# Query heads keep their scale until the exponential, and three gate chunks go ahead of the gate products

## The chip, the cores and the metric

The kernel runs on one core of one Trainium2 chip. The metric is the device time of one execution in microseconds; the time of a version is the median of its runs. One further execution was recorded by the hardware profiler, and every view shown here comes from such a recording. PE is TensorE's matrix unit, PEld its weight loads, DVE is VectorE, ACT is ScalarE, POOL is GpSimd and SP is SyncE, which here only issues transfers.

## The reference, cut to what matters

One layer of a hybrid encoder over 512 tokens of width 2048, in float32. An input projection gives q, k, v, a gate for the attention, and an input and a gate for a recurrent group. Attention has 8 query heads and 2 key/value heads of 128 columns.

```python
q = rms_norm(q.reshape(B, S, N_HEADS, HEAD_DIM), q_norm_w)
k = rms_norm(k.reshape(B, S, N_KV_HEADS, HEAD_DIM), k_norm_w)
q = apply_axial_rope(q, tables)
k = apply_axial_rope(k, tables)
...
s = jnp.einsum('bkgqd,bksd->bkgqs', qb, k_t) * scale
p = jax.nn.softmax(s, axis=-1)
out = jnp.einsum('bkgqs,bksd->bkgqd', p, v_t)
...
mixed = concat([rms_norm(attn_out, attn_norm_w) * silu(g_attn),
                rms_norm(lru_out, lru_norm_w) * silu(g_lru)])
return x + mixed @ w_out
```

Here rms_norm divides a head's 128 values by their root mean square and multiplies by a weight. The root mean square is one number for a token and a head, so it may also be applied to that row of the scores.

## The kernel before

**Matrix products.** Each float32 operand is split into a rounded part ("hi") and the rest ("lo"), both in TensorE's reduced float32 format, and `mm3` (line 151) adds three matmuls: hi·hi, hi·lo, lo·hi. A weight chunk is loaded into one of three `wr` buffers by a transfer that SP issues, ACT rounds it (`wh`, line 223 or 1202) and DVE subtracts (`wl`, line 225 or 1203). A `wr` buffer is free again when that subtraction is done, and the next load into it can be issued only then.

**Stages.** Projection of the recurrent input; the recurrent group itself, laced with further projections; k and v; the two halves of q (`q_proj`, line 1103, four heads each, called from `both`); the attention, laced with gate products (from line 1266); the last gate, the normed output and the output projection. The attention stage runs from about 255 us to 436 us of the profile.

**The heads' norm and rotation.** `norm_rope` (line 541) gets four token tiles with four heads each (two for k). Per tile and head a Square on ACT with an accumulated sum (line 549) gives the sum of squares, `rsqrt_mean` (lines 285 and 286) turns a tile's sums into 1/rms on POOL, and DVE multiplies the tile by it (line 554), multiplies the swapped halves by the sine table in two instructions (line 556), multiplies by the cosine table (line 562) and adds (line 563). The tile `rr` with 1/rms has four buffers.

**The attention.** `attention` (line 667) is a generator with steps d. In a step, PE turns finished weights of two steps before (`turn_weights`, line 631: four transposes and a split by ACT line 578 and DVE line 579, for two token tiles), multiplies weights and values for a head in the even steps (`values`, line 639), turns the q of a later head in the odd ones (`turned`, line 601), and makes two tiles of scores (`weights`, line 607). Each tile of scores goes to `softmax` (line 620): DVE takes the negated maximum of a row (line 623), ACT the exponential with that as its bias and the sum accumulated (line 626), DVE the reciprocal (line 627), POOL the multiplication (line 628). Transposes, scores, turned q and value products share four PSUM banks (`mm`, line 142), in turn: in an odd step two groups of transposes, one turned q and two score tiles take five banks, so the second score tile gets the bank of the first group of transposes.

**The gate products between.** After a score tile PE does one or three units of `gates` (line 1250), four units before the first, as `STEPS` and `weave` say. A unit is six matmuls with 512 columns. Two units make a pair, and the string `PLAN` (line 1248) is the order of the pairs. A `u` is a pair of `gl_units` (line 1159): the recurrent group's gate is formed from seven products of combined blocks, in the order P1, Q6, P2, Q5, Q3, Q7, Q4, of four pairs each. Its weights are 512 KB a pair (two rounded tiles, two subtractions); Q6, Q5, Q3 and Q7 also load 256 KB of combined x (`draw`, line 1172), with one rounding and one subtraction more (`dh` and `dl`, lines 1174 and 1175). A `G` is a pair of `ga_units` (line 1191), the gate of two attention heads: 256 KB, one rounding, one subtraction. An `H` is the same for two more heads. `u` accumulates in the first two of four `pj` banks, `G` and `H` in the other two. From the fifth unit, every second unit also issues a transfer of `out_sums` on POOL's queue, which forms sums of w_out in device memory.

**Who orders what.** PE's order is that of the program. POOL's too, in this stage. ACT, DVE and SP are ordered by a planner from priorities (`tc.high_priority`); each engine then runs its list in order.

Of the kernel before, what the change touches and what calls it, by code (L numbers as in the profile page):

```python
# [11 lines left out]
F32 = mybir.dt.float32  # L12
F32R = mybir.dt.float32r
AF = mybir.ActivationFunctionType
# [3 lines left out]
P = 128  # L18
# [3 lines left out]
NT = SEQ // P  # L22
HD = 128
NH = 8
NKV = 2
G = NH // NKV
# [20 lines left out]
SOON, FIRST = 40, 300  # L47
# [15 lines left out]
def hybrid_kernel(  # L63
# [20 lines left out]
    nc = tc.nc  # L84
# [4 lines left out]
    pools, order = {}, {"left": [], "right": []}  # L89
# [25 lines left out]
    def nm(s):  # L115
        cnt[0] += 1
        return f"{s}_{cnt[0]}"
# [4 lines left out]
    def work():  # L122
        return ("lru", LRU_K2, LRU_B4) if "lru" in pools else ("att", ATT_K2, ATT_B4)

    def k2(dt=F32, shape=(P, SEQ)):
        pool, n, _ = work()
        return pools[pool].tile(list(shape), dt, tag="k2", bufs=n, name=nm("k2"))
# [14 lines left out]
    def mm():  # L142
        return ps.tile([P, SEQ], F32, tag="mm", name=nm("mm"))

    def const(shape, name, dt=F32):
        return cp.tile(list(shape), dt, tag=name, name=name)
# [4 lines left out]
    def mm3(acc, lh, ll, rh, rl, start, stop):  # L151
        nc.tensor.matmul(acc, lh, rh, start=start, stop=False)  # L152
        nc.tensor.matmul(acc, lh, rl, start=False, stop=False)  # L153
        nc.tensor.matmul(acc, ll, rh, start=False, stop=stop)  # L154
# [7 lines left out]
    nc.gpsimd.memset(nhalf, -0.5)  # L162

    nw_st = k2(shape=(KT, P))
    mark = const([P, P], "mark")
    vec_st = const([R_END, P], "vec_st")

    def vec_load():
# [114 lines left out]
    def rsqrt_mean(dst, src, n, width):  # L283

        nc.gpsimd.tensor_scalar(dst, src, 1.0 / n, EPS, op0=ALU.mult, op1=ALU.add)
        nc.gpsimd.tensor_tensor(dst, dst, nhalf[:, :width], op=ALU.pow)
# [75 lines left out]
    def proj_tok(c0, acc):  # L362
        yield from tok_block(acc, w_in, 0, c0, xh, xl, KT)
# [167 lines left out]
    def evac_tok(acc, tile_of):  # L531

        res = []
        with tc.high_priority():
            for t in range(NT):
                e = tile_of()
                nc.scalar.activation(e, acc[t], AF.Identity, scale=rstd[:, t : t + 1])
                res.append(e)
        return res

    def norm_rope(es, nh, tab):

        es = [e[:, : nh * HD].rearrange("p (h d) -> p h d", d=HD) for e in es]
        rs = []
        for e in es:
            r = pools["rot"].tile([P, G], F32, tag="rr", bufs=NT, name=nm("rr"))[:, :nh]
            for h in range(nh):
                sq = pools["rot"].tile([P, HD], F32, tag="sh", bufs=1, name=nm("sh"))
                nc.scalar.activation(sq, e[:, h, :], AF.Square, accum_out=r[:, h : h + 1])  # L549
            rsqrt_mean(r, r, HD, nh)  # L550
            rs.append(r)
        for t, (e, r) in enumerate(zip(es, rs)):
            sq = gbc[:, : nh * HD].rearrange("p (h d) -> p h d", d=HD)
            nc.vector.tensor_mul(e, e, r[:, :, None].broadcast_to([P, nh, HD]))
            for s in range(2):
                nc.vector.tensor_mul(
                    sq.rearrange("p h (a s d) -> p h a s d", s=2, d=32)[:, :, :, s, :],
                    e.rearrange("p h (a s d) -> p h a s d", s=2, d=32)[:, :, :, 1 - s, :],
                    tab[:, t, 1, :].rearrange("p (a s d) -> p a s d", s=2, d=32)[:, None, :, s, :]
                    .broadcast_to([P, nh, 2, 32]),  # L560
                )
            nc.vector.tensor_mul(e, e, tab[:, t, 0, :][:, None, :].broadcast_to([P, nh, HD]))
            nc.vector.tensor_add(e, e, sq)
        return es
# [36 lines left out]
    def turned(rot, h, by=SOON):  # L601

        q = b4(F32R)
        soon(split_ps, turn(rot, h), q[:, 0, :], q[:, 1, :], by=by)
        return q[:, 0, :], q[:, 1, :]

    def weights(q, g, t, by):

        qh, ql = q
        tt = slice(t * P, (t + 1) * P)  # L610
        sc = mm()
        mm3(sc, qh[:, tt], ql[:, tt], kth[g], ktl[g], True, True)
        return soon(softmax, sc, by=by)

    def soon(what, *given, by=SOON):

        with tc.high_priority(by):
            return what(*given)

    def softmax(sc):  # L620

        mx = pools["att"].tile([P, 1], F32, tag="mx", bufs=16, name=nm("mx"))
        nc.vector.tensor_reduce(mx, sc, axis=AX.X, op=ALU.max, negate=True)
        p = k2()
        sm = pools["att"].tile([P, 1], F32, tag="sm", bufs=16, name=nm("sm"))
        nc.scalar.activation(p, sc, AF.Exp, bias=mx, accum_out=sm)
        nc.vector.reciprocal(sm, sm)  # L627
        nc.gpsimd.tensor_scalar(p, p, sm, 0.0, op0=ALU.mult, op1=ALU.add)  # L628
        return p

    def turn_weights(p, t, pth, ptl):
        tt = slice(t * P, (t + 1) * P)
        pt = mm()
        for s in range(NT):
            nc.tensor.transpose(pt[:, s * P : (s + 1) * P], p[:, s * P : (s + 1) * P], ident)  # L635
        p3 = pt.rearrange("p (s q) -> p s q", q=P)
        soon(split_ps, p3, pth[:, :, tt], ptl[:, :, tt])

    def values(h, pth, ptl):

        gs = slice(h // G * HD, (h // G + 1) * HD)
        o = mm()
        for s in range(NT):
            mm3(o, vh[s][:, gs], vl[s][:, gs], pth[:, s, :], ptl[:, s, :], s == 0, s == NT - 1)
        if h % 2 == 0:
            ap_[h // 2] = aring.tile([P, 2, SEQ], F32, name=nm("av"))
        av, asum = ap_[h // 2][:, h % 2, :], sums["a"]
        nc.scalar.copy(av, o)
        if h == 0:
            nc.scalar.activation(asum, av, AF.Square)  # L650
        else:
            sq = k2()
            nc.scalar.activation(sq, av, AF.Square)
            nc.gpsimd.tensor_add(asum, asum, sq)

    def turned_weights():
        return [
            pools["low"].tile([P, NT, SEQ], F32R, tag="pt", bufs=ATT_PT, name=nm("pt"))
            for _ in range(2)
        ]  # L660
# [6 lines left out]
    def attention(rots):  # L667

        pts, ps_ = {0: turned_weights()}, {}
        qs = {h: turned(rots[0], h, FIRST) for h in range(2)}  # L670
        yield 4
        for d in range(2 * NH + 3):
            h, half = divmod(d - 4, 2)
            if h >= 0 and half == 0:
                values(h, *pts.pop(h))
            h, half = divmod(d - 2, 2)
            if 0 <= h < NH:
                if half == 0:
                    pts[h] = pts.get(h) or turned_weights()
                for t in (2 * half, 2 * half + 1):  # L680
                    turn_weights(ps_.pop((h, t)), t, *pts[h])
            h, half = divmod(d, 2)
            if h < NH:
                if half == 1 and h + 2 < NH:
                    qs[h + 2] = turned(rots[(h + 2) // G], (h + 2) % G)
                for e, t in enumerate((2 * half, 2 * half + 1)):
                    ps_[h, t] = weights(qs[h], h // G, t, SOON if d else FIRST)
                    yield STEPS[e]
            elif d < 2 * NH + 2:
                yield 2  # L690
            else:
                yield 0
# [342 lines left out]
    given = {}  # L1035
# [17 lines left out]
    for step in proj_feat(C_XR, a1, first, given):  # L1053
# [8 lines left out]
        c, e = step  # L1062
# [21 lines left out]
    rq, rk = rope_consts()  # L1084
# [16 lines left out]
    rots = []  # L1101

    def q_proj(c0, acc):
        yield from proj_tok(c0, acc)
        rots.append(norm_rope(evac_tok(acc, ev), G, rq))

    def both():
        for n, _ in enumerate(q_proj(C_Q, a4)):
# [127 lines left out]
    def heads_gates(res):  # L1236

        for g in res:
            nc.scalar.activation(g, g, AF.Silu)
        yield  # L1240
        for e, g in enumerate(res):
            dst = ap_[0][:, e, :]
            nc.vector.scalar_tensor_tensor(
                dst, dst, v1(R_AN + e), g, op0=ALU.mult, op1=ALU.mult
            )
            yield

    PLAN = "uuuuG" "uuuuG" "uuuuG" "uuGuuG" "uuGuuG" "uuuuG" "uuuu" "HHHHHHHH"

    def gates():  # L1250
        early, b = [], [pj() for _ in range(4)]
        units = {"u": gl_units(b[:2]), "G": ga_units(0, early, b[2:]), "H": ga_units(1, late, b[2:])}
        todo = iter(())
        for n, unit in enumerate(itertools.chain.from_iterable((u, u) for u in PLAN)):
            done = next(units[unit])
            if n >= 4 and n % 2 == 0:
                next(out_sums, None)
            if done == "Q4":
                todo = itertools.chain(todo, lru_gates(1))
            elif unit == "G" and len(early) == 2 and n == PLAN.rindex("G") * 2 + 1:  # L1260
                todo = itertools.chain(lru_gates(0), heads_gates(early))
# [9 lines left out]
    r = group_rstd([sums["a"]], "r_a", NH * HD)  # L1271
# [31 lines left out]
    acc = []  # L1303
# [74 lines left out]
```

## Time and profile before

| | |
|---|---|
| runs | 649.17, 649.77, 650.11 us; median 649.77 |
| the profiled execution's own time | 650.25 us |
| its span, from the first to the last instruction | 648.1 us |
| mean granted TensorE clock over the span | 0.997 |
| DVE, ACT and POOL busy | 510.2, 379.5 and 136.1 us |
| moved by DMA | 128.19 MB |

The page of a profile gives busy times and the costliest groups of instructions. The view of waits says for whom an engine sat idle. The timeline lists instructions by start, and "x8" is eight of them merged. Matmul ends are modelled and overlap, so PE's speed is read from start to start. The chain of waits goes back from the last instruction, at each step to what released it. The view by stretches gives each engine's busy time and number of instructions, the granted clock, the DMA engines' busy share and GB/s.

### The profile page before, as it was taken

How to read it: one execution, taken by the hardware profiler on the slowest of the kernel's cores; microseconds unless marked ns; L12 is line 12 of the kernel's file. 1: busy time of each engine (PE TensorE's matmuls, PEld its weight loads, DVE VectorE, ACT ScalarE, POOL GpSimd, SP SyncE). 2: the span in 40 equal slices, each digit the busy share in tenths (PEclk: the TensorE clock that was granted, in tenths of full speed). 3: DMA queues.
4: the chain of work that ended last, by engine and by line, in shares of the span. 5: the costliest groups of instructions: out<-in, count | busy, mean ns of one | idle time of the engine just before them, and what ended most of it. 6: DMA issues, size and time to landing. Idle time of an engine off the chain costs nothing.

```text
span 648.1 us, 8952 instructions
## 1 busy us (share of the span) xinstructions
PE 638.3 (98%) x2962; PEld 528.8 (82%) x2962; DVE 510.2 (79%) x894; ACT 379.5 (59%) x699; POOL 136.1 (21%) x173
## 2 busy tenths in 40 slices
PE   8999999999999999979999999999999999999997
PEld 6888888888888888858888888888888888888886
DVE  5877679996799994986768777749937978699994
ACT  3543799489946515765776687745344654443441
POOL 0003303323151300643354334402000000010000
PEclk9999999999999999999999999999999999999999
DMA  8847977897767563597979977853354857586322
GB/s 289 294 135 206 237 199 162 248 251 185 168 181 210 159 209 119 179 271 210 239 214 239 255 217 188 206 147 115 97 182 167 324 167 243 196 280 212 119 95 97
DMA packets 68782, 128.19 MB, mean 198 GB/s; under 512 B 5504, under 2 KB 24320, under 8 KB 68480
## 3 DMA queue, kind: packets, MB, share of 16 engines
q1 hardware_dynamic: 55856, 90.25, 42.5%
q0 software_dynamic: 12704, 37.23, 25.4%
q8 instruction: 23, 0.38, 0.2%
q14 instruction: 23, 0.19, 0.1%
q10 hardware_dynamic: 176, 0.14, 0.1%
HBM read 119.21 MB, written 41.95 MB: 249 GB/s over the span
## 4 chain that ended last, share of the span: by engine, by line
PE 87%; DMA 4%; DVE 3%; ACT 3%; issue 1%; SPq 0%; POOL 0%; ACTq 0%; DVEq 0%
PE pj L152 17%; PE pj L153 17%; PE pj L154 17%; PE mm L984 13%; PE pj L984 11%; PE mm L152 3%; PE mm L154 3%; PE mm L153 3%; DMA wr<-in_w_in_dram 2%; DVE wl L225 1%; PE mm L635 1%; DMA wr<-gs 1%; ACT wh L223 1%; PE mm L255 1%; ACT sh L549 1%
## 5 line engine op out<-in xcount | busy, mean ns | idle before, releaser
L223 ACT CAST wh<-wr 128x512 fp32r<-128x512 f32 x151 | 90.5, 619 | 75.8 <-PE pj L154 30.9
L225 DVE TENSOR_TENSOR wl<-wr,wh 128x512 fp32r<-128x512 f32 (+1 forms) x153 | 105.0, 710 | 26.9 <-ACT wh L223 26.7
L152 PE MATMUL pj<-x,wh 128*128 128x512 f32 x248 | 97.8, 394 | 0.0
L153 PE MATMUL pj<-x,wh 128*128 128x512 f32 x248 | 96.7, 390 | 0.4 <-DVE x L258 0.4
L154 PE MATMUL pj<-x,wl 128*128 128x512 f32 x248 | 96.7, 390 | 0.0
L152 PE MATMUL pj<-wh,x 128*128 128x512 f32 x240 | 94.0, 392 | 0.0
L154 PE MATMUL pj<-wh,x 128*128 128x512 f32 x240 | 93.5, 389 | 0.0
L153 PE MATMUL pj<-wl,x 128*128 128x512 f32 x240 | 93.4, 389 | 0.0
L778 ACT CAST oh<-rw 128x512 fp32r<-128x512 f32 x94 | 56.3, 621 | 38.8 <-PE mm L984 15.5
L779 DVE TENSOR_TENSOR ol<-rw,oh 128x512 fp32r<-128x512 f32 x94 | 61.8, 687 | 10.8 <-ACT oh L778 7.8
L153 PEld LDWEIGHTS pj<-x,wh 128*128 128x128 f32 x248 | 46.6, 188 | 10.1 <-DVE x L258 0.7
L152 PEld LDWEIGHTS pj<-x,wh 128*128 128x128 f32 x248 | 46.6, 188 | 9.8 <-ACT x L257 0.2
L154 PEld LDWEIGHTS pj<-x,wl 128*128 128x128 f32 x248 | 46.5, 188 | 9.8
L154 PEld LDWEIGHTS pj<-wh,x 128*128 128x128 f32 x240 | 45.0, 188 | 9.5
L153 PEld LDWEIGHTS pj<-wl,x 128*128 128x128 f32 x240 | 45.1, 188 | 9.2
L152 PEld LDWEIGHTS pj<-wh,x 128*128 128x128 f32 x240 | 45.1, 188 | 9.1
L984 PE MATMUL mm<-ol,mh 128*128 128x512 f32 (+1 forms) x128 | 49.0, 382 | 0.0
L984 PE MATMUL mm<-oh,ml 128*128 128x512 f32 (+1 forms) x128 | 48.9, 382 | 0.0
L984 PE MATMUL mm<-oh,mh 128*128 128x512 f32 (+1 forms) x128 | 48.9, 382 | 0.0
L916 POOL DMA_DIRECT2D out_dram<-xt x12 | 6.5, 541 | 189.5 <-DVE xt L952 139.1
L628 POOL TENSOR_SCALAR k<-k,sm 128x512 f32<-128x512 f32 x32 | 32.8, 1025 | 61.2 <-DVE sm L627 59.6
L984 PE MATMUL pj<-ol,mh 128*128 128x512 f32 (+1 forms) x104 | 39.7, 382 | 0.0
(238 smaller groups left out, 1342.0 us busy)
## 6 DMA issues: line engine op xcount, KB each, us to landing
wr<-in_w_in_dram SPq DMA_DIRECT2D x59, 512.0 KB, 4.5
rw<-in_w_out_dram SPq DMA_DIRECT2D x63, 256.0 KB, 3.6
gs<-in_w_in_dram POOLq DMA_DIRECT2D x24, 512.0 KB, 6.7
ts<-in_w_out_dram POOLq DMA_DIRECT2D x24, 512.0 KB, 7.8
wr<-gs SPq DMA_DIRECT2D x16, 512.0 KB, 4.7
rw<-ts SPq DMA_DIRECT2D x31, 256.0 KB, 4.4
wr<-in_w_in_dram SPq DMA_DIRECT2D x17, 256.0 KB, 4.5
gs<-gs POOLq DMA_DIRECT2D x8, 512.0 KB, 7.3
```

What stands on the lines that cost most here:

```text
L152: nc.tensor.matmul(acc, lh, rh, start=start, stop=False)
L153: nc.tensor.matmul(acc, lh, rl, start=False, stop=False)
L154: nc.tensor.matmul(acc, ll, rh, start=False, stop=stop)
L223: rounded(hi[:, c], raw[:, k, c])
L225: nc.vector.tensor_sub(lo[:, c], raw[:, k, c], f(hi[:, c]))
L255: nc.tensor.transpose(pt[:, t * P : (t + 1) * P], xc[:, h * n + t, ks], ident)
L549: nc.scalar.activation(sq, e[:, h, :], AF.Square, accum_out=r[:, h : h + 1])
L628: nc.gpsimd.tensor_scalar(p, p, sm, 0.0, op0=ALU.mult, op1=ALU.add)
L778: nc.scalar.copy(hi, src)
L779: nc.vector.tensor_sub(lo, src, f(hi))
L916: (queue or nc.gpsimd).dma_start(of[t * P : (t + 1) * P, os_], xts[g][t][:, cs])
L984: nc.tensor.matmul(bank[key][:, to], lh[:, a, ts_], rh[:, cols], start=i == 0 and j == 0, stop=i == 7 and j == 2,)
```

## The change

Four edits go together. `norm_rope` gets an optional list of tiles for 1/rms; the two calls for q pass tiles of their own (`q_r`, eight of them, kept to the end), and with those given, the tiles of q are not multiplied by 1/rms. `softmax` gets the column of 1/rms of its head and token tile: a new ACT instruction on a 128x1 tile multiplies the negated maximum by it, and the exponential takes it as its scale. `mark`, a tile of which one column is written, gives up the space that the eight tiles take. `PLAN` has three `G` pairs ahead of P1, none inside or after P1 and Q6, and one after P2 and one after Q5; from the 21st pair on it is as before. k is treated as before.

```diff
-    mark = const([P, P], "mark")
+    mark = const([P, P - 16 * NT], "mark")
+    q_r = [const([P, G], f"q_r{i}") for i in range(2 * NT)]
...
-    def norm_rope(es, nh, tab):
+    def norm_rope(es, nh, tab, rs=None):
 
         es = [e[:, : nh * HD].rearrange("p (h d) -> p h d", d=HD) for e in es]
-        rs = []
-        for e in es:
-            r = pools["rot"].tile([P, G], F32, tag="rr", bufs=NT, name=nm("rr"))[:, :nh]
+        given, rs = rs is not None, rs or []
+        for t, e in enumerate(es):
+            if not given:
+                rs.append(pools["rot"].tile([P, G], F32, tag="rr", bufs=NT, name=nm("rr"))[:, :nh])
+            r = rs[t]
             for h in range(nh):
                 sq = pools["rot"].tile([P, HD], F32, tag="sh", bufs=1, name=nm("sh"))
                 nc.scalar.activation(sq, e[:, h, :], AF.Square, accum_out=r[:, h : h + 1])
             rsqrt_mean(r, r, HD, nh)
-            rs.append(r)
         for t, (e, r) in enumerate(zip(es, rs)):
             sq = gbc[:, : nh * HD].rearrange("p (h d) -> p h d", d=HD)
-            nc.vector.tensor_mul(e, e, r[:, :, None].broadcast_to([P, nh, HD]))
+            if not given:
+                nc.vector.tensor_mul(e, e, r[:, :, None].broadcast_to([P, nh, HD]))
...
-    def weights(q, g, t, by):
+    def weights(q, g, t, r, by):
...
-        return soon(softmax, sc, by=by)
+        return soon(softmax, sc, r, by=by)
...
-    def softmax(sc):
+    def softmax(sc, r):
 
         mx = pools["att"].tile([P, 1], F32, tag="mx", bufs=16, name=nm("mx"))
         nc.vector.tensor_reduce(mx, sc, axis=AX.X, op=ALU.max, negate=True)
+        nc.scalar.activation(mx, mx, AF.Identity, scale=r)
         p = k2()
         sm = pools["att"].tile([P, 1], F32, tag="sm", bufs=16, name=nm("sm"))
-        nc.scalar.activation(p, sc, AF.Exp, bias=mx, accum_out=sm)
+        nc.scalar.activation(p, sc, AF.Exp, bias=mx, scale=r, accum_out=sm)
...
-                    ps_[h, t] = weights(qs[h], h // G, t, SOON if d else FIRST)
+                    r = q_r[NT * (h // G) + t][:, h % G : h % G + 1]
+                    ps_[h, t] = weights(qs[h], h // G, t, r, SOON if d else FIRST)
...
-        rots.append(norm_rope(evac_tok(acc, ev), G, rq))
+        n = NT * len(rots)
+        rots.append(norm_rope(evac_tok(acc, ev), G, rq, q_r[n : n + NT]))
...
-    PLAN = "uuuuG" "uuuuG" "uuuuG" "uuGuuG" "uuGuuG" "uuuuG" "uuuu" "HHHHHHHH"
+    PLAN = "GGGuuuu" "uuuu" "uuuuG" "uuuuG" "uuGuuG" "uuuuG" "uuuu" "HHHHHHHH"
```

## The prediction

> **What bounds the kernel now.** I read the page first, then PE's waits, then PE's timeline around the waits, then the chain of waits.
>
> ```profile
> PE 638.3 (98%) x2962; PEld 528.8 (82%) x2962; DVE 510.2 (79%) x894; ACT 379.5 (59%) x699; POOL 136.1 (21%) x173
> ```
>
> PE is busy for 98% of the span. So a change that leaves PE's work alone, as this one does, can only win what PE loses to waits, and what a slower clock after them costs. PE's waits are five:
>
> ```profile
> PE mm L152 <- DVE pt L579: 3.3, 1, 3.3
> PE mm L1023 <- DVE ones L159: 1.0, 1, 1.0
> PE mm L152 <- ACT k L626: 0.9, 1, 0.9
> PE pj L153 <- DVE x L258: 0.4, 1, 0.4
> PE pj L331 <- DVE wh L223: 0.3, 1, 0.3
> ```
>
> Three of them are in the load phase at the start (lines 159, 258 and the first chunk), which the change doesn't touch. The other two, 4.2 us, lie in the attention:
>
> ```profile
> 284.09 0.60 PE L574 MATMUL mm<-ident,ev 128*128 128x128 f32 x4
> 285.62 0.50 PE L152 MATMUL mm<-kt,b 128*128 128x512 f32 x1 [0.93 <-ACT k L626]
> ...
> 287.56 0.39 PE L154 MATMUL pj<-wh,dl 128*128 128x512 f32 x1
> 291.28 0.79 PE L152 MATMUL mm<-kt,b 128*128 128x512 f32 x1 [3.33 <-DVE pt L579]
> ...
> 294.81 0.40 PE L154 MATMUL pj<-wh,dl 128*128 128x512 f32 x1
> 295.04 0.39 PE L152 MATMUL pj<-x,wh 128*128 128x512 f32 x1
> ```
>
> From start to start a matmul takes 0.23 us (294.81 to 295.04). The first wait costs 0.9 to 1.0. The second costs 291.28 - 287.56 - 0.23 = 3.5. Behind it eight matmuls take 294.81 - 291.28 = 3.5 us instead of 8 x 0.23 = 1.8, which is 1.7 more. The view by stretches shows why:
>
> ```profile
> core 0: us, PE busy (x) PEld busy (x) DVE busy (x) ACT busy (x) POOL busy (x), PEclk, DMA share, GB/s
> 285.00:290.00 5.00, 2.33 (x9) 1.61 (x9) 2.13 (x6) 2.32 (x6) 3.68 (x4) 1.00 1.00 346
> 290.00:295.00 5.00, 3.72 (x9) 2.99 (x10) 4.38 (x8) 2.66 (x6) 0.00 (x0) 0.66 1.08 299
> 340.00:360.00 20.00, 20.00 (x99) 16.55 (x99) 15.68 (x28) 12.54 (x27) 8.74 (x10) 1.00 0.95 260
> ```
>
> After the long wait the granted clock is 0.66. In all the place loses 1.0 + 3.5 + 1.7 = 6.2 us, and that is about all that there is to win. Why PE waited stands in the chain:
>
> ```profile
> 262.43 1.27 POOL rr L285
> 263.77 1.02 POOL rr L286
> ...
> 279.44 1.22 DVE wl L225
> 280.68 8.51 DMA wr<-in_w_in_dram
> 289.28 0.63 ACT wh L223
> 289.93 0.69 DVE wl L225
> 290.62 0.61 DVE pt L579
> ```
>
> Read it backwards. The scores at 291.28 wanted a PSUM bank that held transposed weights; DVE had their subtraction (line 579) in its list behind that of a weight chunk (289.93), that chunk had landed at 289.2, its load had been issued only at 280.68, and it was issued so late because DVE freed the buffer only at 280.66. DVE was behind, and POOL's 1/rms for the second half of q was one cause. What DVE did from 255.5 to 287.5, a wait that ends in that stretch being put in whole:
>
> ```profile
> L225 DVE TENSOR_TENSOR wl<-wr,wh 128x512 fp32r<-128x512 f32 x13 | 9.7, 745 | 0.0
> L1175 DVE TENSOR_TENSOR dl<-draw,dh 128x512 fp32r<-128x512 f32 x5 | 3.4, 686 | 0.1
> L554 DVE TENSOR_TENSOR ev<-ev,rr 128x512 f32<-128x512 f32 x4 | 2.8, 689 | 6.2 <-ACT dh L1174 5.0 <-POOL rr L286 1.2
> L1203 DVE TENSOR_TENSOR wl<-wr,wh 128x512 fp32r<-128x512 f32 x2 | 1.4, 687 | 0.3 <-ACT wh L1202 0.3
> ```
>
> **The change, part by part.**
>
> *Multiplications removed.* Eight of 0.69 us leave DVE. The four of the first half of q lie in the projection before, where PE doesn't wait: worth nothing. The other four are 4 x 0.69 = 2.8 us in exactly the stretch where DVE is behind, and the wait for POOL's 1/rms (1.2 us) leaves DVE with them. Sum: 4.0 us.
>
> *Order of the pairs.* The stall lies in the ninth pair (PE is one unit short of the end of Q6). Subtractions for weights by then: before, 4 x 2 for P1, 1 for G, 4 x 3 for Q6, which is 21; after, 3 for three G, 8 for P1, 2 x 3 for half of Q6, which is 17. Four fewer at 0.69 to 0.75 are 2.8 us. The same count for bytes: 2 + 0.25 + 4 x 0.75 = 5.25 MB before, 0.75 + 2 + 2 x 0.75 = 4.25 after. By the 21st pair all of it has been made up, but nowhere is the sum ahead of before: what is moved is only moved later. A G also needs its own two banks, freed by ACT's copies of the last projection; in the old order of ACT they end before the unit that would use those banks, so I price that at nothing; if not, it costs one copy, 0.7 us, once.
>
> So DVE reaches the point of 280.66 some 4.0 + 2.8 = 6.8 us earlier. The load is issued at 273.9, lands at 282.4 even if it takes 8.51 us again, and the rest of the chain (2.0 us from 289.28 to 291.28) ends at 284.4, where PE would want it at 287.8. The margin is 3.4 us; both waits go, since the first one, too, was an exponential whose maximum DVE delivered late. What is late next is the PSUM bank in the odd steps, below.
>
> *The new instruction and the longer exponential.* Rows of the kernel by form:
>
> ```profile
> L626 ACT ACTIVATE k<-mm,mx 128x512 f32<-128x512 f32 x32 | 22.0, 686 | 15.6 <-DVE mx L623 14.2 <-DVE sm L627 1.4
> L1222 ACT ACTIVATE ev<-ev,r_l 128x512 f32<-128x512 f32 x8 | 5.7, 722 | 0.0
> L447 ACT ACTIVATE k<-ev,vec 128x512 f32<-128x512 f32 x8 | 6.5, 814 | 4.3 <-DVE ev L412 4.3
> L1043 ACT ACT_TABLE_LOAD  x1: 1283/1283/1283, 1.2 to 1.2; - x1
> L1043 ACT ACTIVATE table<-ones x1: 202/202/202, 2.5 to 2.5; 128x1 f32<-128x1 f32 x1
> L257 ACT ACTIVATE x<-mm,nw x17: 473/682/689, 4.3 to 38.4; 128x512 fp32r<-128x512 f32 x15, 128x256 fp32r<-128x256 f32 x2
> L386 ACT ACTIVATE lc<-lc x1: 216/216/216, 47.9 to 47.9; 128x16 f32<-128x16 f32 x1
> ```
>
> The same function and shape takes 722 ns with one column operand (line 1222) and 814 with two (line 447): 92 ns for a column. The exponential has one now and gets a second: about 0.78 us instead of 0.69. The 128x1 instruction is bounded from below by the 202 ns of line 1043 (no column operand) and from above by 202 + 92 = 294 with its column; I take 0.29. That is 0.38 us for each of 32 softmaxes, 12 us on ACT in 150 us, in which ACT is two thirds busy (12.5 of 20 us in the last stretch above). A switch of tables would be dear, but there is none: exponential at 2.5, the Identity of line 257 to 38.4, exponential at 47.9, and one load ahead of all of them. In the congested stretch ACT has four fewer roundings (4 x 0.63 by the row of 289.28, 2.5 us) against six longer softmaxes (two in each of the first three steps, 2.3 us), so it comes out even.
>
> The Trainium skill (ScalarE: Activation LUTs, What ACT_TABLE_LOAD costs) gives 186 ns plus 0.833 ns an element without column operands; for one element that is an estimate of 187 against the trace's 202. By it the 32 softmaxes would cost 0.5 us less on ACT; no run here shows this shape with a column yet.
>
> The wait is no new one: the exponential stood behind the same maximum. Queued behind it on ACT are roundings of weights and copies of transposes. The tightest place is an odd step, where the second score tile gets the first transposes' bank 3.4 us after they began:
>
> ```profile
> 345.73 1.03 PE L635 MATMUL mm<-ident,k 128*128 128x128 f32 x8
> 349.13 0.50 PE L152 MATMUL mm<-kt,b 128*128 128x512 f32 x1
> ...
> 346.74 1.07 ACT L578 CAST pt<-mm 128x512 fp32r<-128x512 f32 x2
> ...
> 348.40 1.27 DVE L579 TENSOR_TENSOR pt<-mm,pt 128x512 fp32r<-128x512 f32 x2
> ```
>
> The first of DVE's two subtractions ends half-way, near 349.0: slack 0.1 us. There are five such steps (heads 1 to 5). If a lengthened softmax stands ahead of the copy there, it costs up to 0.38 us, two of them 0.76; five steps at 0.76 are 3.8 at most. At the other end it costs nothing, or gains 0.1 a step where DVE is freer, 0.5 in all. In the rows above ACT's copies are done 0.6 us before DVE begins, so DVE ends last there and ACT has room for a softmax and a half: I take 0.3 us in all, near the lower end.
>
> *The rest.* Shrinking `mark` and keeping eight small tiles moves no work. POOL computes the same 1/rms in the same place in its order; nobody on DVE waits for it, and ACT needs it for the second four heads only four heads later.
>
> *Sum.* 650.25 - 6.2 + 0.3 = 644.35 us for the profiled execution. That one lies 0.48 above the median of the runs, so 643.9 us on the median's scale.
>
> **The rivals.**
>
> *A: the weights are late again, elsewhere.* P1 and Q6 now follow each other with no light pair between, and Q6 wants 0.75 MB a pair. For it: the DMA share is 0.95 to 1.08 in the stretches above. Against it: at 0.95, from 340 to 360, PE doesn't lose anything. Price: one wait as long as that at 291.28, which leaves 643.9 + 3.5 = 647.4, or 649.1 with the clock's 1.7. A shorter one, half of it, would give 645.7. Row: the idle 0.93 left the clock at 1.00, the 3.33 took it to 0.66. The Trainium skill (TensorE: Matmul & The Clock Gate, Part 1: The HAM clock gate) has the clock fall after an idle window of about 3.4 us that runs freely; by it a wait of 3 us can go either way, so 647.4 and 649.1 are both open.
>
> *B: the change doesn't do what it says; the transfer is late, not DVE.*
>
> ```profile
> wr<-in_w_in_dram SPq DMA_DIRECT2D x59, 512.0 KB, 4.5
> ts<-in_w_out_dram POOLq DMA_DIRECT2D x24, 512.0 KB, 7.8
> ```
>
> The load of 280.68 took 8.51 us where the median is 4.5, beside POOL's transfers of 7.8. If the loads are issued earlier but land when those let them, PE waits as before: 649.8. The Trainium skill (DMA: Bandwidth & Descriptors, Issuing engines are not separate DMA queues) has all queues interleave on the same 16 engines, which is this mechanism. Against it: a margin of 3.4 us, and 1 MB less to move by then.
>
> *C: slower, the softmax on PE's path.* Place: the PSUM bank at each of the 16 steps with scores. Price: two softmaxes of 0.38, 0.76 a step, 12.2 us in all; with the 6.2 won, 650.25 + 6.0, on the median's scale 655.8. It decides if the slack of a step is under 0.76 - 6.2 / 16 = 0.37 us on average. For it is the slack of 0.1 above; against it, that in the even steps the fifth bank is that of the value product, which one copy on ACT frees, and that PE shows no second wait on an exponential than that of 285.62.
>
> **How the numbers follow.** Forecast 0.74; A 0.16; B 0.06; C 0.04. Faster or slower begins at 0.2%, 1.3 us, about what a measurement of this kernel can tell from no change. Faster: the forecast and most of A (0.14), 0.88. Same: B and the rest of A, 0.08. Slower: C, 0.04. The range goes down to 642.6 (643.9 less 0.3 + 0.5 of the softmax's bounds and the runs' half spread of 0.5) and up to 647.4, A without the clock's part; it leaves out some 0.17.
>
> **What would show it.** Right: in PE's waits no row of the attention above 0.5 us; a granted clock of 1.00 from 285 to 295; no wait of line 554 for POOL, and the first loads of Q6 landing before ACT wants them; a 128x1 Identity of 0.2 to 0.3 us, exponentials of 0.78, four table loads at line 626 as before. Wrong: a wait over 1 us on a PSUM bank (A if a `wr` transfer ends its chain, C if an exponential does), or the same wait with an earlier issue (B).

## The result and the profile after

The changed kernel takes 644.85 us (644.75 to 645.31) against 649.72 for the kernel before: a ratio of 0.9927, interval 0.9910 to 0.9944. It is 4.9 us faster; the forecast was 643.9, a gain of 5.9. The profiled execution took 644.75 us with a span of 643.0.

The page of the changed kernel, and its view of PE's waits (engine, line, whom it waited for, us in all, times, longest):

```profile
PE 637.2 (99%) x2962; PEld 527.6 (82%) x2962; DVE 508.3 (79%) x886; ACT 392.2 (61%) x733; POOL 132.4 (21%) x173
```

```profile
PE mm L1028 <- DVE ones L159: 1.0, 1, 1.0
PE pj L152 <- DVE ev L1150: 0.6, 1, 0.6
PE pj L152 <- ACT ev L1147: 0.2, 1, 0.2
```

Both waits of the attention are gone, and two others, shorter, have come. They write to `pj`, the banks of the gate products, and they wait for `ev`: what takes a finished product out of its banks, a copy on ACT for P1 (line 1147) and a subtraction on DVE for Q6 (line 1150). The timeline of the changed kernel shows where:

```profile
279.54 0.39 PE L154 MATMUL pj<-wh,x 128*128 128x512 f32 x1
280.18 0.50 PE L152 MATMUL pj<-wh,dh 128*128 128x512 f32 x1 [0.24 <-ACT ev L1147]
...
298.68 0.39 PE L154 MATMUL pj<-wh,dl 128*128 128x512 f32 x1
299.67 0.50 PE L152 MATMUL pj<-wh,x 128*128 128x512 f32 x1 [0.60 <-DVE ev L1150]
```

The operand changes from x to `dh` (P1 ends, Q6 begins) and back (Q6 ends, P2 begins). From start to start the two borders take 0.64 and 0.99 us where a matmul takes 0.23: 0.4 and 0.8 us lost. Before, a `G` pair with banks of its own stood at each of these borders, and PE worked on it while ACT and DVE emptied the banks.

The clock stays up, in the view by stretches (columns as in the prediction):

```profile
285.00:290.00 5.00, 5.00 (x23) 4.10 (x23) 4.62 (x8) 3.72 (x10) 1.85 (x3) 1.00 0.95 183
290.00:295.00 5.00, 5.00 (x27) 4.23 (x27) 2.75 (x6) 3.19 (x7) 2.32 (x3) 1.00 1.04 356
```

And the groups of the changed kernel by form, ACT's part of the softmax and the loads of its tables:

```profile
L630 ACT ACTIVATE k<-mm,mx,q_r 128x512 f32<-128x512 f32 x32 | 24.9, 778 | 1.3
L627 ACT ACTIVATE mx<-mx,q_r 128x1 f32<-128x1 f32 x32 | 9.4, 292 | 4.7 <-DVE mx L626 4.4
L630 ACT ACT_TABLE_LOAD x5 | 6.4, 1283 | 0.1
L1225 ACT ACT_TABLE_LOAD x4 | 5.1, 1283 | 0.1
L1245 ACT ACT_TABLE_LOAD x1 | 1.3, 1283 | 0.0
```

The exponential takes 778 ns and the new instruction 292. Of the loads of ACT's tables in the attention, one stands at the Silu of line 1245 (404.92 us). There are ten in all; before there were eight:

```profile
L626 ACT ACT_TABLE_LOAD x4 | 5.1, 1283 | 0.1
L1219 ACT ACT_TABLE_LOAD x3 | 3.8, 1283 | 0.1
L1239 ACT ACT_TABLE_LOAD x1 | 1.3, 1283 | 0.0
```

To compare versions I take two fixed places in PE's order, the matmuls that begin at 250.10 and 440.20 us in the kernel before, and the time that each version takes from the one to the other. The work between them is the same in all versions, so a difference is what PE loses or wins there. Before it is 190.1 us, after 185.6: 4.5 us less. Of the 5.1 us between the two spans the other 0.7 lies ahead of the first place, which comes 0.7 us earlier: two waits of 0.4 and 0.3 us in the load phase, which the change doesn't touch, did not occur in this execution. What a single place costs is read from the interval between two starts, less 0.227 us for a matmul with 512 columns or 0.109 for a transpose.

| version | median us | ratio to before, interval | PE between the two places, us |
|---|---|---|---|
| before | 649.72 | | 190.1 |
| changed | 644.85 | 0.9927, 0.9910 to 0.9944 | 185.6 |
| norm_only | 645.96 | 0.9937, 0.9923 to 0.9950 | 186.8 |
| plan_only | 647.30 | 0.9958, 0.9946 to 0.9971 | 187.8 |
| cover | 644.34 | 0.9916, 0.9903 to 0.9929 | 184.6 |
| second_half | 646.22 | 0.9946, 0.9925 to 0.9966 | 186.8 |
| cover_second_half | 644.80 | 0.9918, 0.9895 to 0.9942 | 185.2 |
| cover_dve | 644.48 | 0.9923, 0.9897 to 0.9949 | 185.1 |
| three_small | 658.42 | 1.0131, 1.0107 to 1.0155 | 198.8 |
| three_small_ordered | 657.99 | 1.0123, 1.0106 to 1.0139 | 198.1 |
| after_ordered | 656.05 | 1.0090, 1.0076 to 1.0105 | 197.1 |
| cover_ordered | 654.42 | 1.0065, 1.0052 to 1.0078 | 195.0 |
| off_chain | 652.02 | 1.0030, 1.0019 to 1.0042 | 186.1 |
| sums_late | 661.74 | 1.0180, 1.0165 to 1.0195 | 186.6 |

Each ratio is to runs of the kernel before on the same chip. "three_small" to "off_chain" do extra or reordered work on ACT, "sums_late" issues POOL's transfers later; these are probes, not proposals.

### The profile page after: what moved, and what is told of

It is laid out like the page before. It is cut to its first block, busy times and chain, and to the rows that moved or that the text cites. A ratio compares the mean times of both kernels' runs of the same rounds, so it can differ in the third digit from the quotient of the medians.

```text
span 643.0 us, 8959 instructions
## 1 busy us (share of the span) xinstructions
PE 637.2 (99%) x2962; PEld 527.6 (82%) x2962; DVE 508.3 (79%) x886; ACT 392.2 (61%) x733; POOL 132.4 (21%) x173
## 4 chain that ended last, share of the span: by engine, by line
PE 97%; DVE 1%; ACT 1%; issue 0%
PE pj L152 19%; PE pj L154 19%; PE pj L153 19%; PE mm L989 13%; PE pj L989 11%; PE mm L153 3%; PE mm L152 3%; PE mm L154 3%; PE mm L639 2%; PE mm L256 1%; PE pj L332 1%; PE mm L577 1%; PE mm L1233 1%; PE mm L1028 0%; DVE pt L582 0%; PE mm L722 0%
## 5 line engine op out<-in xcount | busy, mean ns | idle before, releaser
L152 PEld LDWEIGHTS pj<-wh,x 128*128 128x128 f32 x240 | 45.1, 188 | 10.1 <-DVE ev L1150 1.0
L632 POOL TENSOR_SCALAR k<-k,sm 128x512 f32<-128x512 f32 x32 | 27.7, 866 | 67.7 <-DVE sm L631 56.2
L989 PE MATMUL pj<-oh,mh 128*128 128x512 f32 (+1 forms) x104 | 39.7, 382 | 0.0
```

The lines of the kernel that those rows point to most:

```text
L989: nc.tensor.matmul(bank[key][:, to], lh[:, a, ts_], rh[:, cols], start=i == 0 and j == 0, stop=i == 7 and j == 2,)
```

## Experiments

### One part of the change at a time: norm_only and plan_only

norm_only is the changed kernel with the old `PLAN`:

```diff
-    PLAN = "GGGuuuu" "uuuu" "uuuuG" "uuuuG" "uuGuuG" "uuuuG" "uuuu" "HHHHHHHH"
+    PLAN = "uuuuG" "uuuuG" "uuuuG" "uuGuuG" "uuGuuG" "uuuuG" "uuuu" "HHHHHHHH"
```

> The changed kernel with the old order of pairs: only the scale of the query heads is moved. Theory (DVE was behind, two parts add up): 4.0 of the 6.8 us by which DVE is ahead remain, the long wait of 3.5 us just goes (margin 0.5), the light pairs still stand between the products, so no wait at their borders: 643.5 to 645.5 us. Rival B (the transfer was late whatever DVE did): the wait stays, 649.7. Rival (the order of pairs did it all, the removed multiplications nothing): 649.7 or up to 1 us above it for the longer softmax.

Measured: 645.96 us, 0.9937, 0.5 above the range that was expected. Most of the gain is there, but the long wait, expected just to go, is still 1.9 us. Its view of waits and its chain:

```profile
PE mm L152 <- DVE pt L582: 1.9, 1, 1.9
```

```profile
274.62 0.24 PE pj L153
274.86 0.02 issue
274.88 0.62 ACT dh L1180
275.50 0.53 ACT wh L224
...
276.75 0.61 DVE wl L226
277.36 0.02 issue
277.38 8.62 DMA wr<-in_w_in_dram
286.00 0.02 issue
...
287.42 0.61 DVE pt L582
288.04 0.04 issue
288.08 0.50 PE mm L152
```

It is the same load as before, issued at 277.4 instead of 280.7 and just as slow. What keeps it from being issued earlier is no longer DVE's list: the chain goes back to a matmul of PE, whose end frees the tile that the next rounding writes. DVE was relieved by 4.0 us, but after 3.3 the next condition is the later one.

plan_only is the kernel before with the new `PLAN`.

> The kernel before with the new order of pairs alone: q is still multiplied by 1/rms. Theory: DVE is ahead by 2.8 us only, so some 0.7 us of the long wait stay, without a slower clock after it; the borders P1 to Q6 and Q6 to P2, which no light pair covers now, cost 0.4 and 0.8 us as in the changed kernel: 645.2 to 646.5 us. Rival (the removed multiplications did it all): 649.7 or above, by 1.2 for the borders, 650.9.

Measured: 647.30 us, 0.9958, 0.8 above the range; its waits:

```profile
PE pj L152 <- ACT ev L1141: 1.4, 2, 1.1
PE mm L152 <- ACT k L626: 1.3, 1, 1.3
...
PE pj L152 <- DVE ev L1144: 0.6, 1, 0.6
```

The wait for the weights, of which 0.7 us was expected to stay, is gone altogether. What stays is the short one for an exponential (1.3, its maximum still late on DVE) and the borders, dearer than in the changed kernel (1.1 + 0.2 at the first one), since ACT has exponentials to do just before and between its two copies. So neither edit did all of it, and neither rival holds: between the two places the scale alone wins 3.3 us, the order alone 2.3, both 4.5. They overlap, since each alone shortens or removes the same wait and with it the slower clock. On top of the scale the order wins 1.2 us there and 1.1 on the medians (645.96 to 644.85), though the intervals of the two ratios overlap.

### Is the transfer late by itself: sums_late

```diff
-            if n >= 4 and n % 2 == 0:
+            if n >= 20 and n % 2 == 0:
                 next(out_sums, None)
```

> The kernel before, with POOL's transfers for the sums of w_out begun at the 21st unit instead of the fifth (the same 32 transfers, later). DVE is behind as before, so the load is issued near 280.7 again, but nothing of POOL's stands beside it. Theory (a joint cause: issued late by DVE and slow in landing): it lands in 4.5 to 5.5 us instead of 8.5, near 285.5, the chain ends near 287.5 and the long wait nearly goes: 644 to 646.5. If DVE alone sets it: 649.7. Rival B says 644 to 646.5 here as the theory does, but 649.7 for the two kernels with one edit each.

Measured: 661.74 us, far outside 644 to 646.5, for a reason outside the question: POOL still had transfers ahead of it when the 1/rms of the attention's output was due, and PE waited 12.8 us for line 286, with a slower clock behind it (0.57 from 449 to 455 us). That lies behind the second of the two places. In the attention itself the answer is there:

```profile
PE mm L297 <- POOL r_a L286: 12.8, 1, 12.8
PE mm L152 <- DVE pt L579: 1.4, 2, 1.1
...
PE mm L152 <- ACT k L626: 0.8, 1, 0.8
```

The wait of 3.3 us is 1.1 without POOL's transfers beside the load, and no clock is lost after it (1.00 from 285 to 300 us). The load, issued at 279.87 us, has landed by 285.68, when ACT rounds it without a wait: at most 5.8 us instead of 8.5. So the long wait had two causes that both were needed: DVE's lateness held the issue back, and the load took 8.5 us. Either one cured is enough to shorten it. That is between the theory and rival B, which named the second cause alone; the two kernels with one edit each show the first.

### The borders: cover

```diff
-    PLAN = "GGGuuuu" "uuuu" "uuuuG" "uuuuG" "uuGuuG" "uuuuG" "uuuu" "HHHHHHHH"
+    PLAN = "GG" "uuuuG" "uuuuG" "uuuuG" "uuuuG" "uuuuG" "uuuuG" "uuuu" "HHHHHHHH"
```

> The changed kernel with two light pairs ahead and one behind each of the first six products (GG, then six times uuuuG, then uuuu). Theory (the new order lost 1.2 us at the two borders that it laid bare, PE waiting for the copies that free the banks of the product before): these waits go, 643.5 to 644.0 us. Rival (what the changed kernel lost against the forecast is the longer softmax on the tight banks): no gain, 644.6 to 645.2; rival (two light pairs ahead don't suffice): a wait for weights in Q6 of 1 us or more, 645 to 648.

Measured: 644.34 us, 0.9916, 0.3 above the range, a span of 642.1; PE's waits in the attention:

```profile
PE mm L152 <- ACT k L630: 0.2, 1, 0.2
PE mm L1233 <- ACT k L630: 0.2, 1, 0.2
```

Both waits for `ev` are gone, and two `G` ahead suffice. Between the two places PE takes 1.0 us less than in the changed kernel, near the 1.2 of the theory. By the runs the gain over the changed kernel, 0.5 us, is not beyond the intervals, so the traces decide here, and not the medians.

### Half the scale, and DVE instead of ACT

second_half leaves 1/rms to the exponential for the second four heads only (`norm_rope` for the first half multiplies as before, and their softmax is the old one). cover_second_half is the same with the order of cover.

```diff
-        rots.append(norm_rope(evac_tok(acc, ev), G, rq, q_r[n : n + NT]))
+        rots.append(norm_rope(evac_tok(acc, ev), G, rq, q_r[:NT] if rots else None))
...
+                    r = q_r[t][:, h % G : h % G + 1] if h >= G else None
```

> The changed kernel with 1/rms left to the exponential for the second four heads alone; the first four are multiplied as before and their softmaxes are as short as before (16 Identities fewer). Theory (only the multiplications beside the start of the attention were in the way): as the changed kernel, 644.3 to 645.2 us, or a little better, since the early softmaxes are shorter. Rival (the multiplications of the first half count as well): between the changed kernel and the one with the order of pairs alone, 646 us.

> The order of pairs that covers the borders of all six products, and 1/rms left to the exponential for the second four heads alone. Theory: the borders' 1.2 us are won and half of the longer softmaxes are gone: 643.0 to 644.3 us, the best of the versions by a few tenths. Rival (two light pairs ahead are too few once the first half's multiplications are back): 645 to 647.

Measured: 646.22 and 644.80 us. Both lie above what the theories expected. The first is slower by 1.4 than the changed kernel, though the intervals overlap. That is the number of its rival, 646, but not its place: where the multiplications are (208 to 250 us) PE loses no more than in the changed kernel. Between the two places it takes 1.2 us more; the borders cost 1.3 (1.2 in the changed kernel), and the tight odd steps of heads 3 and 4 cost 0.3 and 0.5 (0.2, once). With the borders covered half a scale and a whole one are alike within the intervals. So nothing was won by shortening sixteen softmaxes; why second_half loses those tenths in the tight steps stays open, the planner having ordered ACT and DVE anew.

cover_dve is cover with the maximum scaled by DVE:

```diff
-        nc.scalar.activation(mx, mx, AF.Identity, scale=r)
+        nc.vector.tensor_mul(mx, mx, r)
```

> The order of pairs that covers the borders, with the negated maximum multiplied by 1/rms on DVE instead of ACT (32 instructions of 128x1 moved, 0.29 us each on ACT, some 0.15 on DVE by the row of the reciprocals). Theory (what PE still loses in that order are exponentials 0.2 us late, ACT being the later of the two in the later steps): 0.2 to 0.5 us better than with ACT, 643.4 to 644.3. Rival (DVE is the later one in the tight steps): no gain or 0.5 us worse, 644.3 to 645.

Measured: 644.48 us, the same as cover within the intervals. PE's two waits for exponentials become 0.7 us for DVE's splits and 0.3 for an exponential: the rival's picture, at no measurable price. With the maximum scaled on DVE the attention has eight loads of tables, as in the kernel before, and cover has ten.

### Does the softmax's length count: three_small

```diff
         nc.scalar.activation(mx, mx, AF.Identity, scale=r)
+        for _ in range(2):
+            nc.scalar.activation(mx, mx, AF.Identity, scale=1.0)
```

> The changed kernel with two more 128x1 Identity instructions (scale 1) behind the one that it added, so three in place of one for each softmax: 64 more, 0.2 us each by the row of line 1043, 0.4 us a softmax and 13 us on ACT. Theory (the softmax isn't on PE's path except in a few tight steps): under 2 us slower than the changed kernel, 644.5 to 646.8 us. Rival C (the softmax's length counts at each of 16 steps): 644.9 + 12.8 = 657 us.

Measured: 658.42 us, 13.6 slower than the changed kernel. Rival C, with 657, seems to be right. But the loss is not spread evenly over the steps. From 255 to 408 us PE loses about 8 us (2 in the changed kernel), most of it in six places of 0.8 to 1.8, and another 8 lie at one place:

```profile
408.79 0.39 PE L154 MATMUL pj<-wh,x 128*128 128x512 f32 x1
411.60 0.33 PE L1235 MATMUL mm<-ident,ev 128*128 128x128 f32 x1 [2.42 <-ACT ev L1230]
414.48 0.90 PE L1235 MATMUL mm<-ident,ev 128*128 128x128 f32 x3 [2.56 <-ACT ev L1230]
...
416.46 0.63 PE L152 MATMUL pj<-wh,x 128*128 128x512 f32 x1
416.89 0.63 PE L153 MATMUL pj<-wl,x 128*128 128x512 f32 x1
```

PE waits to transpose the recurrent group's gate, which ACT has not scaled. ACT's timeline in the same kernel tells why:

```profile
407.50 1.28 ACT L1227 ACT_TABLE_LOAD   x1
408.80 0.72 ACT L1227 ACTIVATE ev<-ev,rstd 128x512 f32<-128x512 f32 x1
...
411.56 1.28 ACT L632 ACT_TABLE_LOAD   x1
412.86 0.78 ACT L632 ACTIVATE k<-mm,mx,q_r 128x512 f32<-128x512 f32 x1
...
413.72 0.71 ACT L1230 ACTIVATE ev<-ev,r_l 128x512 f32<-128x512 f32 x1
...
414.54 1.28 ACT L1247 ACT_TABLE_LOAD   x1
```

A Silu, an exponential, a Silu again, and each needs its own table. The planner, seeing longer softmaxes, laid single exponentials between the Silus of the gates. There are 14 loads of tables in this attention, ten in the changed kernel, eight before.

### The order of exponentials and Silus held fixed

Three kernels tie each exponential behind the last Silu of the program's order and each Silu behind the last exponential: the changed kernel (after_ordered), cover (cover_ordered) and three_small (three_small_ordered). `in_order` stands in place of `nc.scalar.activation` at the exponential and the three Silus:

```diff
+    def in_order(kind, *given, **named):
+        other = table_use.get("silu" if kind == "exp" else "exp")
...
+            with tc.issue_after(other.ins):
+                ins = nc.scalar.activation(*given, **named)
+        table_use[kind] = ins
```

> The changed kernel, with each exponential told to come behind the last Silu of the program's order and each Silu behind the last exponential, so that ACT changes its table four times in the attention instead of ten (6 x 1.28 = 7.7 us less on ACT). Theory (the changed kernel loses 0.4 + 0.8 at the borders of products, which this doesn't touch, and some 0.5 us in places where ACT is late): 0 to 0.5 us better, 644.3 to 645.0. Rival (ACT's spare is what is short all over the attention): over 1 us better, under 643.9.

> The same two orders on top of the order of pairs that covers the borders. Theory: PE's last waits there were for exponentials, 0.2 us each, and an idle place near 414; they go: 643.3 to 644.3 us, equal to or 0.5 better than without. Rival (the fixed order makes exponentials wait for Silus whose gates are late): worse, 645 to 647.

> The kernel with three small Identities for each softmax, with the fixed order of exponentials and Silus. That kernel had 14 changes of table in the attention against 10, and most of PE's loss of 16 us lay where Silus and exponentials alternate. Theory (the longer softmax made the planner alternate, and the table loads, not the softmax's length, cost the time): four changes of table, 10 x 1.28 = 12.8 us less on ACT, the loss falls to that of the changed kernel and 1 to 3 us more: 645.5 to 648.5. Rival C (the length itself, 0.4 us at each step): 656 to 658 as without.

Measured: 656.05, 654.42 and 657.99 us, with four loads of tables each. Against the kernels without the fixed order the first two are 11.2 and 10.1 us slower, more than either expectation had. All three lose it mainly at one place; in after_ordered:

```profile
PE mm L1245 <- ACT ev L1240: 8.0, 1, 8.0
```

The Silus of the gate now stand behind the last exponentials, and PE, whose order is fixed, waits 8 us for them and runs at a slower clock after (0.61 from 405 to 415 us). Fewer loads of tables were no gain here, since the Silus came too late. The number of three_small_ordered alone, 657.99, is that of rival C. But the comparison that the three were made for can be read: with the order fixed, the 64 additional instructions cost 657.99 - 656.05 = 1.9 us (1.0 between the two places) instead of 13.6. That the long wait hides the rest is not the reason: from 255 to 400 us, ahead of it, they cost 1.6 us. So the softmax's length as such is a small part of what cost time; the order that the planner makes of it, its table loads included, is the larger. How those 13.6 us divide between the loads (four more, 5.1 us of ACT) and the rest of the order stays open.

off_chain puts the same two instructions for each softmax on a tile that nobody waits for:

```diff
+        for _ in range(2):
+            nc.scalar.activation(mark[:, 1:2], ones[:, 0:1], AF.Identity, scale=1.0)
```

> The changed kernel with two more 128x1 Identities for each softmax as well, but on a tile of their own that nothing waits for: the same 13 us on ACT, not between maximum and exponential; ten changes of table as in the changed kernel. Theory (the table loads cost the time, not ACT's time in small pieces): 645 to 647.5 us. Rival (ACT's time as such): 656 to 658 as with three in the chain.

Measured: 652.02 us, and no answer. Depending on nothing in the attention, all 64 were moved by the planner to 2.6 to 21.4 us, where PE waited 5.2 us for ACT in the load phase. Between the two places PE takes 0.5 us more than in the changed kernel.

## Why the prediction was right, and where it was not

**What there was to win.** Right: the prediction named one place with 6.2 us. cover, the best version here, wins 5.5 between the two places, and from the second of them to the end the kernels before and after take the same time (207.9 and 208.0 us).

**The removed multiplications, 4.0 us of DVE's time.** Right in kind. Alone they won 3.3 us between the two places (norm_only). The wait of DVE for POOL's 1/rms is gone. The size of the step was taken too simply: the load can be issued 6.8 us earlier only if nothing but DVE holds it. In norm_only it came forward by 3.3, and then PE's own progress was the later condition. In the changed kernel this did not show, since Q6 comes later.

**The order of the pairs.** This is the step that failed: "nowhere is the sum ahead of before: what is moved is only moved later". The bytes and subtractions were counted rightly, and the loads of Q6 were in time though they were not faster. What the sentence left out is that a `G` between two products had a second use: it kept PE busy with other banks while ACT and DVE emptied those of the finished product. The prediction looked for that very thing at the first `G` (the banks freed by the last projection's copies) and not at the borders from which the `G` pairs were taken. It measured 0.4 + 0.8 = 1.2 us, and cover, which puts them back, takes 1.0 us less between the two places. That is most of what the attention's gain of 4.5 us lacks to the forecast 5.9. The profiled executions, 5.5 us apart, come closer to the forecast than the attention did, but by luck: 0.7 us of theirs lies in the load phase, which the change doesn't touch.

**The new instruction and the longer exponential.** Right: 0.29 and 0.78 us were said, 292 and 778 ns measured, 12 us more on ACT said, 32 x (0.292 + 0.778 - 0.686) = 12.3 measured. The tight odd steps cost 0.2 us once (343.4 us). Wrong was "four table loads at line 626 as before". There are five there and ten in all against eight. No load stands at the Identity itself, as argued; the two more come with the order in which the planner lays ACT's work, and cover_dve, without the Identity on ACT, has eight again. In the changed kernel they were hidden; three_small shows what they are part of when they are not.

The Trainium skill (ScalarE: Activation LUTs, What ACT_TABLE_LOAD costs) adds about 93 ns for a column operand to 186 and 0.833 an element, an estimate of 280 for the new instruction; the trace's 292 agrees. For a switch of tables it has about 2.66 us, of which half is a drain. Here the trace differs: in the changed kernel a load at 404.92 takes 1.28 us, the Identity before it ends at 404.90 and the Silu after it begins at 406.21, so a switch costs 1.3 us of ACT, and by the page's figure the two more loads would have taken an estimated 2.7 us more of ACT than they did.

**The rivals.** A did not occur: no wait for weights in the attention of the changed kernel. B was half a cause, not a rival: loads stayed slow (the one issued at 284.98 took 9.5 us) and PE did not wait for them. C did not occur either: 644.85 us, not 655.8, and no wait of PE for an exponential. three_small_ordered speaks against it as it was put, too; but a longer softmax can cost far more than nothing by way of the order, and the prediction had not thought of that way.

## What to carry to other kernels

Where work is moved away from a place, ask what it covered there, bank by bank, and not only what it brings where it goes: a light piece between two accumulations hides their copies. When a wait has two causes in a row, a fix of one brings it forward only to the next condition, so look up what else the late instruction needs before crediting the whole shift. And where a planner orders an engine with table loads, count the loads after each edit: here 0.4 us more in each softmax went with exponentials laid between Silus.

## What was not expected of the hardware

The clock. A wait of 1.9 us (norm_only) left it at 1.00 from 283 to 300 us. In three_small two waits of 2.4 and 2.6 us, with one recorded transpose between, brought matmuls from 0.23 to 0.43 us from start to start (416.46 to 416.89), about half speed, though neither was as long as the 3.3 us of the kernel before. The granted clock is 1.00 from 412.3 to 412.7 us and 0.50 from 412.8 to 413.2, so it fell inside the second wait. The Trainium skill (TensorE: Matmul & The Clock Gate, Part 1: The HAM clock gate) has an idle window of about 3.4 us; two waits close together seem to count as one here, which these runs show in this one place only. Within the kernels, the stretches at half clock in the clock records of the traces last 3.41 us in the kernel before, 6.83 in three_small, 10.24 in after_ordered and 13.65 in sums_late: one, two, three and four times the same length.
